# Attention summed by parts, and split projection weights kept in DRAM

## The chip, the core and the metric

The kernel runs on one core of a Trainium2 chip. The metric is the time of one execution in microseconds of the device (us), taken as the median of several runs. A core has a matrix engine (TensorE, PE in the profile; its weight loads are listed as PEld), a vector engine (VectorE, DVE), an activation engine (ScalarE, ACT), a general engine (GpSimd, POOL) and SyncE (SP), whose queue issues nearly all DMAs of this kernel. Work arrays lie in SBUF (128 partitions); matrix products land in PSUM.

## What is computed

One layer of a hybrid decoder block on 2048 tokens of width 1024, in float32. The normalised and modulated input `h` is projected by one matrix `w_in` of 4232 columns; the columns feed three mixers, whose gated outputs go through `w_out` and are added to the input.

```python
proj = h @ w_in                     # u, v, z of a gMLP; q, k, v, o, z, i, f of an mLSTM; q, k, v, z of attention
# stick-breaking attention, 6 heads of 64, by blocks of 128 queries:
z = einsum('bthd,bshd->bhts', qb, kb) * scale
log_not = where(strict, log_sigmoid(-z), 0.0)           # strict: s < t
suffix = cumsum(log_not, reverse=True) - log_not
a = where(strict, exp(log_sigmoid(z) + suffix), 0.0)
out = einsum('bhts,bshd->bthd', a, vb)
```

So the weight of key s is sigmoid(z_s) times the product of sigmoid(-z) over the later keys. With B_s, the product of sigmoid(-z) from s to the end, it is B_(s+1) - B_s.

## The kernel before, in words

The sequence is 16 tiles of 128 tokens, taken in three blocks of 5, 5 and 6 tiles (`BLOCKS`). For a block, the modulated input lies transposed in SBUF, split into a high and a low part (`hT`), and so do the projection's weights: every product with a projection is three matmuls, high by high, high by low and low by high.

**Weights.** `weights` yields the columns of one projection as 8 tiles of 128 rows (`wt`, tag `wr`, 11 buffers). `load_w` brings 256 rows into a staging tile (`st`, 2 buffers); ACT copies the high part, and DVE and POOL in turn subtract it to make the low part (L180, L181). A block calls it for 11 projections: three times q, k, v of a pair of heads (`c_proj`), and eight others. So every weight is loaded and split three times, once in a block: 33 calls, 264 tiles.

**Attention.** Heads are taken in pairs, p = 0, 1, 2. `c_proj` makes q, k and v of a pair, tile by tile; `c_evac` normalises q and k, turns them into `Qst` and `Kst` and puts v, high and low part, into `Vst`. It works in two pieces, the second one tile later. K and V of earlier blocks come from DRAM (`k_d`, `v_d`). `stick` then runs units (a query tile, a head, up to four key tiles, from the last keys to the first), 240 in all, in a pipeline of four steps: `front` makes the scores (PE), two sigmoids `bb` and `be` (ACT), masks the diagonal tile in both (POOL), runs the product from right to left over `bb` (a scan on DVE, 513 columns with a 1 at the end), and multiplies `be` by the shifted `bb`, in turn on DVE and POOL; `middle` transposes the result (PE) and splits it into `aT` (ACT high, DVE low); `back` multiplies with `Vst`; `fin` folds the parts and stores the tile (`yc`).

**Order.** While attention of a pair runs, the other projections of the block are woven between its steps (`interleave`, by estimated cost). The order on each engine comes from a scheduler that follows priorities: weights stand far ahead of the rest (`HIGH`), attention a little (`STK`). On the chip each engine and the SP queue then run their instructions in that fixed order. After the third block the output phase does the mLSTM's chunks and the output projection; nothing of the change is in it.

Of the kernel before, what the change touches and what calls it, by code (L numbers as in the profile page):

```python
# [17 lines left out]
P = 128  # L18
# [6 lines left out]
WMAX = 392  # L25
STK = -30
T5 = 6
OFF = dict(au=0, av=256, az=512, bq=768, bk=1152, bv=1536, bo=1920, bz=2304, bi=2688,
           cq=2696, ck=3080, cv=3464, cz=3848)
# [3 lines left out]
def hybrid_block_kernel(ctx: ExitStack, tc: tile.TileContext, x, c, norm_g, w_ada, b_ada, w_in,  # L33
# [8 lines left out]

# [1 line left out]
    qkT_d = dram.tile([768, SEQ], F32, name="qkT_d")  # L44
# [7 lines left out]
    k_d = [dram.tile([P, 2, SEQ], F32, name=f"k_d{p}") for p in range(3)]  # L52
    v_d = [dram.tile([P, NT, 2, P], F32, name=f"v_d{p}") for p in range(3)]

# [1 line left out]
    ident = const.tile([P, P], F32, name="ident")  # L56
# [35 lines left out]

# [1 line left out]
    rs = ExitStack()  # L94
# [50 lines left out]
    def mod_x(i, c0, c1, eng=None):  # L145
        """normalised and modulated, in place"""
        xc = x_cols(i, c0, c1)
        nc.vector.scalar_tensor_tensor(xc, xc, xtiles[i][1], hscale[:, c0:c1], ALU.mult, ALU.mult)
        (eng or nc.gpsimd).tensor_tensor(xc, xc, hshift[:, c0:c1], ALU.add)
# [10 lines left out]

    ntag = [0]

    def load_w(src, segs, kp):
# [8 lines left out]
    def weights(src, segs, kps=range(KT // 2), staged=None):  # L172
        """hi and lo parts of the given columns, one tile per 128 rows"""
        W = sum(w for _, w in segs)
        tiles = []
        for kp in kps:
            st = staged[kp] if staged else load_w(src, segs, kp)
            for a in range(2):
                wt = wr_p.tile([P, 2, WMAX], F32R, tag="wr", name=f"wr{ntag[0]}_{kp}_{a}")
                nc.scalar.copy(wt[:, 0, :W], st[:, a, :W])  # L180
                (nc.vector if a == 0 else nc.gpsimd).tensor_tensor(  # L181
                    wt[:, 1, :W], st[:, a, :W], wt[:, 0, :W].bitcast(F32), ALU.subtract)
                tiles.append(wt)
        ntag[0] += 1
        return tiles
# [4 lines left out]

# [1 line left out]
    ht_p = lw.enter_context(tc.tile_pool(name="ht", bufs=1))  # L192
# [4 lines left out]
    crow = tmp.tile([8, P], F32, tag="t512", bufs=T5, name="crow")  # L197
    brow = [stk.tile([P, 512], F32, tag="bb", bufs=4, name=f"brow{n}") for n in range(4)]
    for n in (2, 0, 3, 1):
        nc.gpsimd.memset(brow[n], 0.0)  # L200
    g_bc = [stk.tile([P, 512], F32, tag="be", bufs=3, name=f"g_bc{n}") for n in range(2)]

# [41 lines left out]

# [1 line left out]
    NB0 = BLOCKS[0]  # L246
# [22 lines left out]
    def hT_half(i, j, hh):  # L269
        """half of the rows of tile j of hT, hi and lo parts"""  # L270
        cols = slice(j * P, (j + 1) * P)
        ks = slice(hh * 4, hh * 4 + 4)
        pt = (pat.tile([P, 4, P], F32, tag="at", name=f"pt{i}_{hh}") if i < BLOCKS[0] else
              pproj.tile([P, 512], F32, tag="proj", name=f"pt{i}_{hh}").rearrange("p (k t) -> p k t", k=4))
        for k in range(4):
            kk = hh * 4 + k
            nc.tensor.transpose(pt[:, k, :], x_cols(i, kk * P, (kk + 1) * P), ident)
        nc.scalar.copy(hT[:, 0, ks, cols], pt)
        nc.vector.tensor_tensor(hT[:, 1, ks, cols], pt, hT[:, 0, ks, cols].bitcast(F32), ALU.subtract)  # L279

    def proj_tc(ps, wt, j, W, ks=range(KT)):
        """psum[t, cols] of t tile j of the block"""
        cols = slice(j * P, (j + 1) * P)
        for k in ks:
            nc.tensor.matmul(ps, lhsT=hT[:, 0, k, cols], rhs=wt[k][:, 0, :W], start=k == 0, stop=False)  # L285
            nc.tensor.matmul(ps, lhsT=hT[:, 0, k, cols], rhs=wt[k][:, 1, :W], start=False, stop=False)  # L286
            nc.tensor.matmul(ps, lhsT=hT[:, 1, k, cols], rhs=wt[k][:, 0, :W], start=False, stop=k == KT - 1)  # L287
            yield 3 * W / 2.4

# [1 line left out]
    def c_proj(b, t0, nb, p):  # L291
# [20 lines left out]
    def c_evac(b, t0, p, j, ps):  # L312
        i = t0 + j
        if p == 0:
# [7 lines left out]
        nc.gpsimd.tensor_tensor(rr, rr, neghalf[:, 0:4], ALU.pow)  # L322
        nc.scalar.copy(Vst[:, i, :, 0:64], ps[:, 256:384].rearrange("p (h d) -> p h d", h=2))
        nc.vector.tensor_tensor(Vst[:, i, :, 64:128], ps[:, 256:384].rearrange("p (h d) -> p h d", h=2),
                                Vst[:, i, :, 0:64].bitcast(F32), ALU.subtract)
        qk = tmp.tile([P, 4, 2, 64], F32, tag="t512", bufs=T5, name=f"qk{p}_{i}")
# [5 lines left out]
        for a in range(4):  # L332
# [7 lines left out]
        nc.vector.scalar_tensor_tensor(Qst[:, j, 1], pt[:, 0:2, :], gq, Qst[:, j, 0].bitcast(F32),  # L340
                                       ALU.mult, ALU.subtract)
        if b < len(BLOCKS) - 1:
            nc.sync.dma_start(k_d[p][:, :, i * P:(i + 1) * P], ks.bitcast(F32))
            nc.sync.dma_start(v_d[p][:, i], Vst[:, i].bitcast(F32))

    def stick(p, t0, nb):
# [11 lines left out]
        st = {}  # L358
        st_count = []

        def front(u):
# [6 lines left out]
            nc.tensor.matmul(z[:, :w], lhsT=Qst[:, j, 1, h, :], rhs=kk, start=False, stop=True)  # L368
            bb = stk.tile([P, 513], F32, tag="bb", bufs=4, name=f"bb{nm}")
            be = stk.tile([P, 512], F32, tag="be", bufs=3, name=f"be{nm}")  # L370
            nc.gpsimd.memset(bb[:, w:w + 1], 1.0)  # L371
            nc.scalar.activation(bb[:, :w], z[:, :w], AF.Sigmoid, scale=-1.0)  # L372
            nc.scalar.activation(be[:, :w], z[:, :w], AF.Sigmoid)  # L373
            if s1 == i + 1:
                nc.gpsimd.affine_select(out=bb[:, w - P:w], in_=bb[:, w - P:w], pattern=[[-1, P]],  # L375
                                        compare_op=ALU.is_gt, fill=1.0, base=0, channel_multiplier=1)
                nc.gpsimd.affine_select(out=be[:, w - P:w], in_=be[:, w - P:w], pattern=[[-1, P]],
                                        compare_op=ALU.is_gt, fill=0.0, base=0, channel_multiplier=1)
            rev = bb[:, 0:w + 1][:, ::-1]
            nc.vector.tensor_tensor_scan(rev, rev, rev, carry.get((i, h), 1.0), ALU.mult, ALU.bypass)  # L380
            carry[i, h] = bb[:, 0:1]
            eng = nc.gpsimd if len(st_count) % 2 else nc.vector
            st_count.append(0)
            eng.tensor_tensor(be[:, :w], be[:, :w], bb[:, 1:w + 1], ALU.mult)  # L384
            st[u] = [be, None]
            return 2 * w / 2.4

        def middle(u):
            i, j, h, s0, s1 = u
            nm = f"{p}_{i}_{h}_{s0}"  # L390
            be = st[u][0]
            nb_ = s1 - s0
            at = pat.tile([P, 4, P], F32, tag="at", name=f"at{nm}")
            for s in range(nb_):
                nc.tensor.transpose(at[:, s, :], be[:, s * P:(s + 1) * P], ident)  # L395
            aT = stk.tile([P, 4, 2, P], F32R, tag="aT", bufs=3, name=f"aT{nm}")
# [23 lines left out]
        def fin(u):  # L420
# [6 lines left out]
            yc = stk.tile([P, P], F32, tag="yc", bufs=1, name=f"yc{p}_{i}")  # L427
            nc.scalar.copy(yc, py[:, 0:P])
            nc.sync.dma_start(y_d[i * P:(i + 1) * P, 256 + p * P:256 + (p + 1) * P], yc)
# [10 lines left out]

# [1 line left out]
    def bqk_proj(t0, nb, half):  # L442
# [71 lines left out]

# [1 line left out]
    def a_proj(t0, nb, p):  # L516
# [37 lines left out]

# [1 line left out]
    def gating():  # L556
# [62 lines left out]

# [1 line left out]
    def bc4(ap, n):  # L621
# [31 lines left out]
    def first_chunk():  # L653
        """chunk 0 of the mLSTM ahead of the output phase: its gated output and the state after it"""
        big = [tmp.tile([P, D], F32, tag="xt", name=f"m0_{n}") for n in range(2)]
# [37 lines left out]

# [1 line left out]
    def gate_gemv():  # L695
# [137 lines left out]

# [1 line left out]
    rs.close()  # L835
# [46 lines left out]
    def mlstm(i):  # L882
        """numerator and denominator of chunk i, state after it"""
        qk2, vb = loaded[i][0:2]
# [31 lines left out]
    def mixed(i):  # L916
        """the gated outputs of the three mixers, [t, c]"""
        gt, y, xt = loaded[i][2:]
# [42 lines left out]
    def chunk_ahead(i):  # L961
        """chunk i from its scores to the turned outputs"""
        yield from mlstm(i)
        mixed(i)
        yield
        yield from turned(i)
# [66 lines left out]
```

## Time and profile before

| | |
|---|---|
| median of 3 runs | 1531.31 us (1530.76 to 1535.02) |
| span of the profiled execution, first to last instruction | 1527.0 us |
| instructions | 25375 |

The profiled execution's own time is known as its span; what lies around the span, the start and the end of the program, is taken as the difference to the median, 4.3 us. Stretches below are in us from the span's start. The first block runs to some 356 us (its last projection is mixed with the loading of the next block's x), the second to some 720, the third to 1262, and then the output phase. A share of busy time is an average; an engine's instruction can be busy and yet be held up by another's use of a resource.

### The profile page before, as it was taken

The page shows a single profiled execution, that of the slowest core. Times are in us where ns is not written, and L with a number is a line of the kernel's source. Part 1 is how long each engine was busy: PE and PEld are TensorE (multiplying, and loading weights), DVE is VectorE, ACT ScalarE, POOL GpSimd, SP SyncE. Part 2 cuts the span into 40 slices and gives each one's busy share as a digit, 9 for nine tenths or more (in the row PEclk, how much of TensorE's full clock was granted, in tenths as well). Part 3 has the DMA queues.
Part 4 walks back from the last instruction along what each step waited for, and adds up shares of the span by engine and source line. Part 5 has one row for each costly group of instructions (what it writes and reads, how often), then busy time and mean ns, then how long its engine had stood idle before and what let it go on. Part 6 is the DMA issues. An engine that isn't in the chain of part 4 may idle for free.

```text
span 1527.0 us, 25375 instructions
## 1 busy us (share of the span) xinstructions
PE 1413.2 (93%) x8468; PEld 1307.1 (86%) x8468; DVE 1123.3 (74%) x1866; ACT 749.6 (49%) x1832; POOL 757.2 (50%) x1228
## 2 busy tenths in 40 slices
PE   5899999889889999988898899999998978999998
PEld 3789999889878999977898699989898956888887
DVE  6787555775997677699699986879968797544444
ACT  2365444454655455557366755656545565211210
POOL 4364544664445544666344554645535246534442
PEclk8899999999999999999999999999999999999999
DMA  9433423334435422523322124112230154546551
GB/s 325 130 92 100 121 80 87 95 109 122 133 93 140 136 69 74 141 53 111 103 63 74 41 63 124 46 48 76 78 89 18 62 189 120 196 128 190 149 158 67
DMA packets 170595, 163.89 MB, mean 107 GB/s; under 512 B 23610, under 2 KB 146904, under 8 KB 170464
## 3 DMA queue, kind: packets, MB, share of 16 engines
q1 hardware_dynamic: 170240, 162.24, 36.1%
q8 instruction: 67, 1.10, 0.3%
q14 instruction: 64, 0.52, 0.1%
q0 software_dynamic: 224, 0.02, 0.0%
HBM read 124.58 MB, written 37.64 MB: 106 GB/s over the span
## 4 chain that ended last, share of the span: by engine, by line
PE 53%; DVE 25%; issue 7%; DMA 6%; POOL 5%; ACT 4%; SPq 0%; DVEq 0%; POOLq 0%; ACTq 0%
DVE bb L380 9%; PE po L946 4%; PE po L948 4%; PE po L947 4%; PE av L410 3%; PE pc L287 3%; DMA st<-in_w_in_dram 3%; PE pc L285 3%; PE pc L286 3%; PE at L395 3%; DVE acc L467 2%; DVE aT L398 2%; PE pg L286 2%; DVE be L384 2%; PE pg L285 2%
## 5 line engine op out<-in xcount | busy, mean ns | idle before, releaser
L380 DVE TENSOR_TENSOR_SCAN bb<-bb,bb 128x513 f32<-128x513 f32 x144 | 198.9, 1382 | 18.4 <-ACT bb L372 18.0
L384 POOL TENSOR_TENSOR be<-be,bb 128x512 f32<-128x512 f32 (+3 forms) x120 | 135.3, 1127 | 125.2 <-DVE bb L380 65.5
L181 POOL TENSOR_TENSOR wr<-st,wr 128x384 fp32r<-128x384 f32 (+1 forms) x132 | 158.4, 1204 | 61.8 <-ACT wr L180 60.0
L180 ACT CAST wr<-st 128x384 fp32r<-128x384 f32 (+1 forms) x264 | 127.3, 522 | 113.0 <-DMA st<-in_w_in_dram 103.2
L410 PE MATMUL av<-aT,Vst 128*128 128x256 f32 x816 | 148.1, 298 | 30.4 <-DVE aT L398 20.8
L410 PEld LDWEIGHTS av<-aT,Vst 128*128 128x128 f32 x816 | 120.6, 192 | 47.5 <-DVE aT L398 30.5
L398 DVE TENSOR_TENSOR aT<-at,aT 128x512 fp32r<-128x512 f32 (+3 forms) x240 | 142.0, 596 | 24.0 <-ACT aT L397 23.6
L372 ACT ACTIVATE bb<-z 128x512 f32<-128x512 f32 (+3 forms) x240 | 131.1, 547 | 53.4 <-PE z L368 47.4
L397 ACT CAST aT<-at 128x512 fp32r<-128x512 f32 (+3 forms) x240 | 126.8, 529 | 51.7 <-PE at L395 50.4
L395 PE MATMUL at<-ident,be 128*128 128x128 f32 x816 | 133.3, 278 | 16.6 <-DVE Qst L340 7.3
L285 PE MATMUL pc<-wr,hT 128*128 128x384 f32 (+1 forms) x384 | 136.0, 356 | 7.2 <-DVE hT L279 6.2
L287 PE MATMUL pc<-wr,hT 128*128 128x384 f32 (+1 forms) x384 | 136.8, 356 | 2.6 <-DVE hT L279 2.6
L181 DVE TENSOR_TENSOR wr<-st,wr 128x384 fp32r<-128x384 f32 (+1 forms) x132 | 103.9, 787 | 47.8 <-ACT wr L180 47.5
L286 PE MATMUL pc<-wr,hT 128*128 128x384 f32 (+1 forms) x384 | 134.7, 351 | 0.0
L373 ACT ACTIVATE be<-z 128x512 f32<-128x512 f32 (+3 forms) x240 | 132.6, 552 | 0.0
L395 PEld LDWEIGHTS at<-ident,be 128*128 128x128 f32 x816 | 98.4, 142 | 28.2 <-DVE aT L398 11.1
L380 DVE TENSOR_TENSOR_SCAN bb<-bb 128x129 f32<-128x129 f32 (+3 forms) x96 | 95.7, 997 | 17.4 <-POOL bb L375 14.5
L946 PE MATMUL po<-wo,yT 128*128 128x512 f32 x256 | 104.8, 409 | 0.3 <-ACT yT L935 0.3
L947 PE MATMUL po<-wo,yT 128*128 128x512 f32 x256 | 102.3, 399 | 0.7 <-POOL wo L853 0.7
L948 PE MATMUL po<-wo,yT 128*128 128x512 f32 x256 | 101.4, 399 | 0.0
L371 POOL MEMSET bb<- 128x1 f32 x240 | 23.4, 98 | 150.6 <-DVE bb L380 98.8
L367 PE MATMUL z<-Kst,Qst 128*128 128x512 f32 (+3 forms) x240 | 93.7, 392 | 3.8 <-ACT be L373 3.7
(272 smaller groups left out, 4098.7 us busy)
## 6 DMA issues: line engine op xcount, KB each, us to landing
st<-in_w_in_dram SPq DMA_DIRECT2D x180, 128.0 KB, 2.4
st<-in_w_in_dram SPq DMA_DIRECT2D x48, 384.0 KB, 3.3
st<-in_w_in_dram SPq DMA_DIRECT2D x48, 192.0 KB, 2.6
wad<-in_w_ada_dram SPq DMA_DIRECT2D x8, 1024.0 KB, 7.3
xo<-in_x_dram SPq DMA_DIRECT2D x16, 512.0 KB, 3.6
out_dram<-o SPq DMA_DIRECT2D x31, 256.0 KB, 2.8
xt<-in_x_dram SPq DMA_DIRECT2D x15, 512.0 KB, 4.4
qk<-qkT_d SPq DMA_DIRECT2D x15, 384.0 KB, 7.5
```

Source lines behind the costliest of these rows:

```text
L181: (nc.vector if a == 0 else nc.gpsimd).tensor_tensor(wt[:, 1, :W], st[:, a, :W], wt[:, 0, :W].bitcast(F32), ALU.subtract)
L285: nc.tensor.matmul(ps, lhsT=hT[:, 0, k, cols], rhs=wt[k][:, 0, :W], start=k == 0, stop=False)
L286: nc.tensor.matmul(ps, lhsT=hT[:, 0, k, cols], rhs=wt[k][:, 1, :W], start=False, stop=False)
L287: nc.tensor.matmul(ps, lhsT=hT[:, 1, k, cols], rhs=wt[k][:, 0, :W], start=False, stop=k == KT - 1)
L380: nc.vector.tensor_tensor_scan(rev, rev, rev, carry.get((i, h), 1.0), ALU.mult, ALU.bypass)
L384: eng.tensor_tensor(be[:, :w], be[:, :w], bb[:, 1:w + 1], ALU.mult)
L395: nc.tensor.transpose(at[:, s, :], be[:, s * P:(s + 1) * P], ident)
L398: nc.vector.tensor_tensor(aT[:, :nb_, 1, :], at[:, :nb_, :], aT[:, :nb_, 0, :].bitcast(F32), ALU.subtract)
L410: nc.tensor.matmul(flat(av), lhsT=Vst[:, s0 + s, h, :], rhs=flat(aT[:, s]), start=(s0 + s == i), stop=(s0 + s == 0))
L946: nc.tensor.matmul(po, lhsT=yT[:, 0, k, :], rhs=wo[k][:, 0, cs], start=k == 0, stop=False)
L947: nc.tensor.matmul(po, lhsT=yT[:, 0, k, :], rhs=wo[k][:, 1, cs], start=False, stop=False)
L948: nc.tensor.matmul(po, lhsT=yT[:, 1, k, :], rhs=wo[k][:, 0, cs], start=False, stop=k == KT - 1)
```

## The change

Attention: `be`, its mask and the product are left out. The weighted sum over s of (B_(s+1) - B_s) v_s is summed by parts: the output is v of the query's tile's last row plus the sum over s of B_s times (v_(s-1) - v_s). So `front` has one sigmoid and the scan, over 512 columns; `middle` transposes `bb` itself; `c_evac` puts the differences of neighbouring rows of v into `Vst`, for which a copy of v is moved by one partition with a DMA, and the first row comes from the last row of the tile before, through DRAM (`vl_d`); and `fin` adds the last row, spread over all partitions by a DMA (`vlast`).

Weights: the first block stores every split tile to DRAM; in the second and third block a tile is loaded from there, both parts at once, and staging and split are left out.

```diff
     def weights(src, segs, kps=range(KT // 2), staged=None):
         W = sum(w for _, w in segs)
         tiles = []
+        key = segs[0][0]
+        made = split.setdefault(key, {})
         for kp in kps:
+            if kp * 2 in made:
+                for k in (2 * kp, 2 * kp + 1):
+                    wt = wr_p.tile([P, 2, WMAX], F32R, tag="wr", name=f"wr{ntag[0]}_{k}")
+                    nc.sync.dma_start(wt[:, :, :W].bitcast(F32), made[k])
+                    tiles.append(wt)
+                continue
             st = staged[kp] if staged else load_w(src, segs, kp)
             for a in range(2):
                 wt = wr_p.tile([P, 2, WMAX], F32R, tag="wr", name=f"wr{ntag[0]}_{kp}_{a}")
...
+                made[2 * kp + a] = dram.tile([P, 2, W], F32, name=f"w_d{key}_{2 * kp + a}")
+                nc.sync.dma_start(made[2 * kp + a], wt[:, :, :W].bitcast(F32))
                 tiles.append(wt)
...
     def c_evac(b, t0, p, j, ps):
...
-        nc.scalar.copy(Vst[:, i, :, 0:64], ps[:, 256:384].rearrange("p (h d) -> p h d", h=2))
-        nc.vector.tensor_tensor(Vst[:, i, :, 64:128], ps[:, 256:384].rearrange("p (h d) -> p h d", h=2),
-                                Vst[:, i, :, 0:64].bitcast(F32), ALU.subtract)
+        vt = tmp.tile([P, P], F32, tag="vt", name=f"vt{p}_{i}")
+        nc.scalar.copy(vt, ps[:, 256:384])
+        nc.sync.dma_start(vl_d[p * NT + i:p * NT + i + 1, :], vt[P - 1:P, :])
+        dv = tmp.tile([P, P], F32, tag="dv", name=f"dv{p}_{i}")
+        nc.sync.dma_start(dv[1:P, :], vt[0:P - 1, :])
+        if i == 0:
+            nc.gpsimd.memset(dv[0:1, :], 0.0)
+        else:
+            nc.sync.dma_start(dv[0:1, :], vl_d[p * NT + i - 1:p * NT + i, :])
...
         yield
...
+        nc.gpsimd.tensor_tensor(dv, dv, vt, ALU.subtract)
+        dv2 = dv.rearrange("p (h d) -> p h d", h=2)
+        nc.scalar.copy(Vst[:, i, :, 0:64], dv2)
+        nc.gpsimd.tensor_tensor(Vst[:, i, :, 64:128], dv2, Vst[:, i, :, 0:64].bitcast(F32), ALU.subtract)
...
         def front(u):
...
-            bb = stk.tile([P, 513], F32, tag="bb", bufs=4, name=f"bb{nm}")
-            be = stk.tile([P, 512], F32, tag="be", bufs=3, name=f"be{nm}")
-            nc.gpsimd.memset(bb[:, w:w + 1], 1.0)
+            bb = stk.tile([P, 512], F32, tag="bb", bufs=BB, name=f"bb{nm}")
             nc.scalar.activation(bb[:, :w], z[:, :w], AF.Sigmoid, scale=-1.0)
-            nc.scalar.activation(be[:, :w], z[:, :w], AF.Sigmoid)
             if s1 == i + 1:
                 nc.gpsimd.affine_select(out=bb[:, w - P:w], in_=bb[:, w - P:w], pattern=[[-1, P]],
                                         compare_op=ALU.is_gt, fill=1.0, base=0, channel_multiplier=1)
-                nc.gpsimd.affine_select(out=be[:, w - P:w], in_=be[:, w - P:w], pattern=[[-1, P]],
-                                        compare_op=ALU.is_gt, fill=0.0, base=0, channel_multiplier=1)
-            rev = bb[:, 0:w + 1][:, ::-1]
+                if h == 0:
+                    vlast[i] = stk.tile([P, P], F32, tag="vlast", name=f"vlast{p}_{i}")
+                    nc.sync.dma_start(vlast[i], vl_d[p * NT + i:p * NT + i + 1, :].broadcast_to([P, P]))
+            rev = bb[:, 0:w][:, ::-1]
             nc.vector.tensor_tensor_scan(rev, rev, rev, carry.get((i, h), 1.0), ALU.mult, ALU.bypass)
             carry[i, h] = bb[:, 0:1]
-            eng = nc.gpsimd if len(st_count) % 2 else nc.vector
-            st_count.append(0)
-            eng.tensor_tensor(be[:, :w], be[:, :w], bb[:, 1:w + 1], ALU.mult)
-            st[u] = [be, None]
+            st[u] = [bb, None]
...
         def middle(u):
...
-                nc.tensor.transpose(at[:, s, :], be[:, s * P:(s + 1) * P], ident)
+                nc.tensor.transpose(at[:, s, :], bb[:, s * P:(s + 1) * P], ident)
...
         def fin(u):
...
-            nc.scalar.copy(yc, py[:, 0:P])
+            nc.vector.tensor_tensor(yc, py[:, 0:P], vlast.pop(i), ALU.add)
```

`BB` is 6; `vt` and `dv` have two buffers, `vlast` two. The start of the program uses `bb`'s buffers where it used `be`'s.

## Rows read from the trace of the kernel before

**Rows 1.** The page, busy time: us, share of the span, instructions.

```profile
PE 1413.2 (93%) x8468; PEld 1307.1 (86%) x8468; DVE 1123.3 (74%) x1866; ACT 749.6 (49%) x1832; POOL 757.2 (50%) x1228
```

**Rows 2.** Stretches: length, busy us (x) of PE, PEld, DVE, ACT, POOL; clock, DMA share, GB/s.

```profile
69.00:382.00 313.00, 298.01 (x1830) 289.56 (x1829) 209.03 (x400) 156.65 (x429) 165.98 (x287) 0.98 0.36 100
382.00:494.00 112.00, 99.56 (x632) 91.43 (x631) 101.79 (x160) 62.83 (x155) 58.50 (x102) 0.98 0.42 120
494.00:612.00 118.00, 118.00 (x736) 114.83 (x735) 85.47 (x144) 65.66 (x166) 56.89 (x103) 1.00 0.35 97
612.00:767.00 155.00, 138.66 (x838) 131.84 (x837) 121.81 (x202) 83.68 (x215) 88.21 (x139) 0.98 0.36 101
767.00:914.00 147.00, 134.31 (x811) 124.63 (x810) 134.89 (x207) 98.28 (x209) 69.56 (x125) 0.98 0.19 56
914.00:1086.00 172.00, 168.90 (x1076) 161.72 (x1075) 140.40 (x219) 105.48 (x249) 88.25 (x151) 1.00 0.24 68
1086.00:1216.00 130.00, 122.46 (x743) 116.32 (x742) 99.70 (x172) 70.19 (x178) 57.19 (x112) 0.97 0.22 61
1216.00:1262.00 46.00, 35.60 (x225) 28.47 (x224) 43.61 (x54) 31.69 (x68) 18.90 (x36) 0.96 0.53 189
1262.00:1527.00 265.00, 252.91 (x1428) 215.05 (x1428) 137.35 (x243) 54.18 (x127) 121.88 (x126) 0.98 0.48 145
```

**Rows 3.** What PE waits for from 316 to 1262 us: us in total, times, longest.

```profile
PE av L410 <- DVE aT L398: 20.0, 20, 2.6
...
PE pc L285 <- DVE hT L279: 6.2, 3, 4.8
...
PE pv L286 <- DVE wr L181: 2.6, 2, 2.4
```

**Rows 4.** The scan's line: durations in ns, min/median/max.

```profile
L380 DVE TENSOR_TENSOR_SCAN bb<-bb,bb x144: 1268/1278/3400, 114.7 to 1257.9; 128x513 f32<-128x513 f32 x144
```

**Rows 5.** Timeline from 716 us: start, duration, engine, line.

```profile
716.10 2.70 POOL L149 TENSOR_TENSOR xt<-xt,hshift 128x1024 f32<-128x1024 f32 x1
...
716.49 3.40 DVE L380 TENSOR_TENSOR_SCAN bb<-bb,bb 128x513 f32<-128x513 f32 x1
```

**Rows 6.** Groups of instructions: busy us, mean ns | idle before, releasers.

```profile
L373 ACT ACTIVATE be<-z 128x512 f32<-128x512 f32 (+3 forms) x240 | 132.6, 552 | 0.0
...
L416 DVE TENSOR_TENSOR avt<-av,avs 128x128 f32<-128x128 f32 x96 | 26.6, 277 | 25.3 <-ACT avs L414 25.1
...
L533 POOL TENSOR_TENSOR gu<-tb 128x128 f32<-128x128 f32 x32 | 19.8, 618 | 24.4 <-DVE tb L532 23.3 <-PE pa L287 0.8
...
L324 DVE TENSOR_TENSOR Vst<-pc,Vst 128x128 fp32r<-128x128 f32 x48 | 13.3, 281 | 2.1 <-ACT Vst L323 2.1
```

**Rows 7.** The product of be and bb alone: length, busy us (x) of DVE, POOL.

```profile
382.00:494.00 112.00, 6.69 (x12) 14.19 (x12) 0.98 0.42 120
767.00:914.00 147.00, 14.73 (x20) 24.43 (x19) 0.98 0.19 56
1216.00:1262.00 46.00, 6.87 (x9) 12.43 (x10) 0.96 0.53 189
```

**Rows 8.** The weights' low parts alone: the same columns.

```profile
382.00:494.00 112.00, 8.24 (x12) 16.77 (x12) 0.98 0.42 120
767.00:914.00 147.00, 10.73 (x12) 16.71 (x12) 0.98 0.19 56
```

**Rows 9.** The DMA view: queue's packets, MB, share; loads by size, us to landing.

```profile
q1 hardware_dynamic: 170240, 162.24, 36.1%
...
st<-in_w_in_dram SPq DMA_DIRECT2D x48, 384.0 KB, 3.3
st<-in_w_in_dram SPq DMA_DIRECT2D x48, 192.0 KB, 2.6
```

**Rows 10.** What the DMA queue on SP waits for: us, times, longest.

```profile
SPq L167 <- POOL wr L181: 171.4, 57, 32.4
```

**Rows 11.** One q-k-v projection of block 1: columns as in the stretches above.

```profile
494.00:519.00 25.00, 25.00 (x152) 24.46 (x151) 11.79 (x25) 9.71 (x27) 10.41 (x14) 1.00 0.50 150
```

More of the change, by code (lines that the diff above doesn't have):

```diff
@@ L27 @@
 T5 = 6
+BB = 6
 OFF = dict(au=0, av=256, az=512, bq=768, bk=1152, bv=1536, bo=1920, bz=2304, bi=2688,
@@ L53, in hybrid_block_kernel @@
     v_d = [dram.tile([P, NT, 2, P], F32, name=f"v_d{p}") for p in range(3)]
+    vl_d = dram.tile([3 * NT, P], F32, name="vl_d")
     ident = const.tile([P, P], F32, name="ident")
@@ L161, in hybrid_block_kernel @@
     ntag = [0]
+    split = {}
     def load_w(src, segs, kp):
@@ L197, in hybrid_block_kernel @@
     crow = tmp.tile([8, P], F32, tag="t512", bufs=T5, name="crow")
-    brow = [stk.tile([P, 512], F32, tag="bb", bufs=4, name=f"brow{n}") for n in range(4)]
+    brow = [stk.tile([P, 512], F32, tag="bb", bufs=BB, name=f"brow{n}") for n in range(4)]
     for n in (2, 0, 3, 1):
         nc.gpsimd.memset(brow[n], 0.0)
-    g_bc = [stk.tile([P, 512], F32, tag="be", bufs=3, name=f"g_bc{n}") for n in range(2)]
+    g_bc = [stk.tile([P, 512], F32, tag="bb", bufs=BB, name=f"g_bc{n}") for n in range(2)]
     def ada_load(half):
@@ L358, in stick @@
         st = {}
-        st_count = []
+        vlast = {}
         def front(u):
@@ L390, in middle @@
             nm = f"{p}_{i}_{h}_{s0}"
-            be = st[u][0]
+            bb = st[u][0]
             nb_ = s1 - s0
```

## The prediction

> **What bounds the kernel now.** I read the page's busy times first, then the busy times by stretch, then what TensorE waits for, then the timeline of one long wait. TensorE (PE) is busy for 93% of the span [rows 1], so its work, which the change leaves alone, sets a floor. The stretches say how far above it the kernel runs [rows 2]. In 494 to 612 us PE is busy all 118.0 us with 736 instructions: 0.160 us each, PE at its own pace. At that pace the other stretches would need, from their counts: 69 to 382, 293.4 of 313 us (19.6 over); 382 to 494, 101.3 of 112 (10.7); 612 to 767, 134.3 of 155 (20.7); 767 to 914, 130.0 of 147 (17.0); 914 to 1086, nothing over; 1086 to 1216, 119.1 of 130 (10.9); 1216 to 1262, 36.1 of 46 (9.9). Together 88 to 89 us that PE isn't at its pace. The output phase, 1262 to 1527, isn't touched.
>
> Three of these are VectorE's (DVE's): it is busy 101.8 of 112, 134.9 of 147 and 43.6 of 46 us, above PE's need in each. The waits agree: PE's largest is the `av` matmul for the low part `aT` that DVE makes, 20.0 us [rows 3]. In the other stretches over PE's pace DVE is at 0.67 to 0.79, and PE also waits for `hT` (6.2 us), which comes with a new block of x. Only few waits are for split weights (2.6 us in the largest row), so the splits harm PE through the engines that they occupy, not by being late.
>
> DVE is also longer at its work than the work takes. A scan of 513 columns has a median of 1278 ns and a maximum of 3400 [rows 4]. The timeline has that maximum: POOL's addition runs from 716.10 for 2.70 us, the scan starts at 716.49 and ends at 719.89, about 1.1 us after POOL [rows 5]. POOL work that reads SBUF can hold up a DVE instruction with two SBUF operands.
>
> **What the change removes.** (a) The second sigmoid, `be`: 240 ACT instructions, 132.6 us [rows 6]; ACT isn't the bound, so alone it is worth nothing, but the score buffer comes free one activation sooner. `bb` gets six buffers for its four and `be`'s three; it now lives until its transposes, one unit longer, which six cover. (b) The product of `be` and `bb`, every other one on DVE: 6.7, 14.7 and 6.9 us of DVE in the three DVE stretches, and 14.2, 24.4 and 12.4 us of POOL [rows 7]. (c) The second and third splits of the weights: in two of these stretches 8.2 and 10.7 us of DVE, 16.8 and 16.7 of POOL [rows 8]; the third has none.
>
> DVE's need falls to 101.8 - 6.7 - 8.2 = 86.9 us in the first and 134.9 - 14.7 - 10.7 = 109.5 in the second, both under PE's need (101.3 and 130.0), so their 10.7 and 17.0 us can come back whole; in the last, 43.6 - 6.9 = 36.7 us stays level with PE's 36.1, and I take 7 of 9.9. That is 35 us. The other stretches hold 51 us over PE's pace, in which DVE gets lighter but x's loads and the chain through `hT` stay, and block 0 keeps its splits. Bounds 0 and 51; no row parts them, so half, 26. Gain: 61 us.
>
> **What it adds.** (d) In the evacuation of q, k and v one DVE subtraction from PSUM (281 ns) goes, and the 48 additions of `vlast` come to DVE; the nearest, `avt`, takes 277 ns [rows 6]. Even. That addition can wait for its broadcast DMA, with the next scans queued behind it on DVE; four units lie between issue and use, so nothing. (e) POOL gets two subtractions of 128x128 per tile, 96 in all: at most the 618 ns of `gu` [rows 6], 59 us, less than (b) and (c) free. The first waits for the shifted copy; behind it on POOL stand the next tile's `rr` and the attention's selects.
>
> (f) **The weights in blocks 1 and 2** come as 176 tiles of 384 KB straight into `wr`, which has 11 buffers of which 8 are in use: three tiles ahead, where the staging held four more. One tile feeds three matmuls, 0.48 us. The fourth tile's buffer comes free 0.48 us into the last row tile of the projection before, and is wanted at 3.84 + 1.44 = 5.28 us. A 384 KB load lands 3.3 us after issue and one of 192 KB in 2.6 [rows 9], so a further tile costs about 2 x 0.7 = 1.4 us. The eighth lands at 0.48 + 3.3 + 4 x 1.4 = 9.4 us and is wanted at 7.2: 2.2 us late. Upper bound 22 x 2.2 = 48 us; lower 0, where attention's matmuls lie between a projection's, as in most stretches. I take eight, the six q-k-v projections and two more, 18 us, less 3 us of waits for splits that go [rows 3]: 15 us. Each load also waits in SP's queue behind whatever is there; SP stands up to 32.4 us at a weight load today, for a split [rows 10]. In block 0 the 88 stores (35 MB) follow the splits on the same queue; the queue moved 162.24 MB in 36.1% of the engines' time [rows 9], so they are 117 us of all 16 engines, and 69 to 382 us goes from a share of 0.36 to 0.73: still hidden, behind PE, and if that cover went a projection would start late as in the other blocks.
>
> (g) **The shift.** Per tile SP issues three more DMAs: the last row of v out, that row of the tile before in, and 127 rows of 512 B moved by one partition. No row has a DMA of 127 rows. By [rows 9], 0.361 x 16 x 1527.0 us over 170240 packets is 51.8 ns for a packet of 953 B, 18.4 B/ns for an engine. Spread over 16 engines the shift holds each 0.2 to 0.4 us; if one engine carries it, by bytes 3.5 us, by packets 6.6. A q-k-v projection of block 1 has five tiles in 25 us at a DMA share of 0.50 [rows 11]: that engine has 2.5 us of other work in a tile's 5.0. Lower bound of the cost 0; the upper is the second rival's. Its packets are the smallest kind, nearest to the lower end, where two buffers of `vt` and `dv` absorb most: I take 8 us.
>
> The Trainium skill (DMA: Bandwidth & Descriptors, "Why a DMA increments its semaphore by 16 and not by 1") says that a DMA uses the largest number of engines up to 16 that divides its slowest dimension, and names 127 partitions as using one. No row here shows it. By that rule the shift's row of the sum would lie between the 30 and 123 us of the second rival; by a spread over 16 it would be 0.
>
> **Sum.** -61 + 15 + 8 = -38 us on the profiled span of 1527.0: 1489, and with the 4.3 us by which the median of the runs (1531.31) stands above that span, **1493 us**.
>
> **Rivals.**
> 1. *All of the slack comes back and both DMA costs are hidden.* 35 + 51 = 86 us: 1445. For it: the stretch 494 to 612 shows that attention and projection can interleave at PE's pace with DVE at 0.72. Against: `hT` and x.
> 2. *The shift is the new bound, slower.* Place: the nine q-k-v projections. If one engine carries it, a tile needs 2.5 + 3.5 to 6.6 = 6.0 to 9.1 us of that engine in 5.0: 1.0 to 4.1 us over. POOL waits for `dv`, so `rr` of the next tiles, hence `qk` and the scores' operands, come late; the weights that follow on the same queue too. Two tiles in each of nine groups find free buffers; 30 are left: 30 to 123 us. It decides when it passes 61 - 15 = 46 us, 1.5 us a tile, a shift of 4.0 us. Middle: 76 - 46 = +30, 1561 us. Against: 512 B packets should be shorter than the mean one.
> 3. *The gain is eaten by the weights.* Every one of 22 projections 2.2 us late (48 us), and the 26 us do not come: -35 + 45 = +10, 1541 us. For it: three tiles of lead and SP's order. Against: attention's matmuls fill in.
> 4. *Costs and gain cancel:* 61 us against 30 for the shift (the lower end of rival 2) and 14 late projections, 31 us: 1531.
>
> **Chances.** What a measurement of this kernel can tell from no change is some 0.3%, 4.6 us. Forecast with its neighbourhood (1470 to 1520): 0.52. Rival 1: 0.15. Rival 4: 0.10, most of it within 0.3%. Rival 2: 0.15. Rival 3: 0.08. So faster 0.68, the same 0.08, slower 0.24. The range goes from rival 1 to a little past rival 3 and the lower part of rival 2: 1444 to 1550; for the forecast alone 1470 to 1520.
>
> **What would show it.** Right: in 382 to 494 and 767 to 914 PE reaches 0.160 us an instruction with DVE under 0.85; scans with few long ones; no wait of PE for `wr` above 2 us a projection; the shift landing in under 4 us. The sum is wrong if PE waits for `wr`<-DMA in sums of 30 us or more (rival 3), if POOL's idle time before the subtraction of `dv` adds up to tens of us and the q-k-v projections grow past 25 us (rival 2), or if DVE stays above 0.9 busy although lighter.

## The result, and the profile after

The changed kernel takes **1551.01 us** (median of four runs, 1548.09 to 1552.60) against 1533.16 for the kernel before on the same chip: a ratio of 1.0119, 95% interval [1.0098, 1.0140], slower by 1.2%. The forecast was 1493, with a range to 1550. The time lies 10 us from the middles of two rivals, 1541 of the third (the gain is eaten by the weights) and 1561 of the second (the shift is the new bound); the waits below tell them apart.

The page after has its busy times first (us, share of the span, instructions), then the main hardware queue's packets, MB and share of 16 engines, then the leading groups of the chain that ended last:

```profile
PE 1423.9 (92%) x8468; PEld 1318.7 (85%) x8468; DVE 942.6 (61%) x1658; ACT 577.4 (37%) x1416; POOL 490.2 (32%) x783
...
q1 hardware_dynamic: 199994, 237.90, 47.8%
...
PE av L429 4%; PE at L414 4%; PE po L965 3%; PE po L967 3%; PE po L966 3%; DMA dv<-vt 3%; DMA wr<-w_d 2%; DMA dv<-vl_d 2%; PE z L391 2%; PE z L392 2%; DVE bb L402 2%; PE pa L298 2%; PE pa L299 2%; PE pa L300 2%; PE pg L299 1%
```

Against [rows 1] the change did what it says: DVE lost 181 us of work, ACT 172, POOL 267; PE has the same 8468 instructions. The time still rose, and the chain names transfers of `dv`, a tile that the kernel before hasn't got. Two of the stretches of [rows 2] in which DVE stood above PE's need (same columns and the same times from the start of the span, so not quite the same work):

```profile
382.00:494.00 112.00, 104.60 (x665) 98.77 (x664) 82.69 (x149) 46.88 (x117) 26.33 (x56) 0.97 0.60 195
767.00:914.00 147.00, 136.54 (x819) 128.53 (x818) 105.98 (x185) 72.63 (x155) 29.80 (x62) 0.97 0.32 101
```

DVE is at 0.74 and 0.72 where it was at 0.91 and 0.92. What the engines wait for (us in total, times, longest) tells what took its place:

```profile
ACT Vst L364 <- POOL dv L362: 170.0, 44, 7.5
...
POOL dv L362 <- DMA dv<-vt: 93.5, 21, 8.6
...
POOL dv L362 <- DMA dv<-vl_d: 54.7, 17, 5.0
```

POOL stands 148 us, in 38 of 48 tiles, before the subtraction that needs the shifted copy; ACT stands 170 us behind POOL, 3.9 us a time. PE's largest wait is a new one, `PE pq L352 <- DVE qk L346: 14.0, 10, 3.9`: it waits to turn the scaled q and k (`qk`), which come late. For a stored weight it waits only 3.6 us at most at one place (`PE pb L472 <- DMA wr<-w_d`, 3.8 us in total), so it isn't the third rival.

**One place in detail**, the end of the second q-k-v projection of block 1. The timeline (start, duration, what; in brackets the idle time before and its releaser):

```profile
541.79 0.46 POOL L362 TENSOR_TENSOR dv<-dv,vt 128x128 f32<-128x128 f32 x1 [3.96 <-issue]
542.28 0.30 ACT L364 CAST Vst<-dv 128x128 fp32r<-128x128 f32 x1 [4.64 <-POOL dv L362]
542.48 0.38 ACT L331 ACTIVATE sq<-pc 128x256 f32<-128x256 f32 x1
542.65 0.47 POOL L365 TENSOR_TENSOR Vst<-dv,Vst 128x128 fp32r<-128x128 f32 x1 [0.41 <-ACT Vst L364]
...
543.15 0.34 SPq L368 DMA_DIRECT2D v_d<-Vst  x1
...
543.58 0.58 SPq L185 DMA_DIRECT2D wr<-w_d  x1
544.22 0.45 SPq L338 DMA_DIRECT2D vl_d<-vt  x1
544.72 0.69 DVE L346 TENSOR_TENSOR qk<-pc,rr 128x512 f32<-128x512 f32 x1 [1.41 <-POOL rr L335]
544.75 4.85 SPq L185 DMA_DIRECT2D wr<-w_d  x7
545.46 0.66 PE L352 MATMUL pq<-ident,qk 128*128 128x128 f32 x4 [1.59 <-DVE qk L346]
...
547.35 0.69 PE L298 MATMUL pg<-wr,hT 128*128 128x384 f32 x1 [0.88 <-DMA wr<-w_d]
...
549.56 0.69 PE L298 MATMUL pg<-wr,hT 128*128 128x384 f32 x1 [0.89 <-DMA wr<-w_d]
549.65 0.67 SPq L340 DMA_DIRECT2D dv<-vt  x1
...
558.87 0.46 POOL L362 TENSOR_TENSOR dv<-dv,vt 128x128 f32<-128x128 f32 x1 [6.11 <-DMA dv<-vt]
562.87 0.45 POOL L362 TENSOR_TENSOR dv<-dv,vt 128x128 f32<-128x128 f32 x1 [3.54 <-DMA dv<-vl_d]
...
563.35 0.30 ACT L364 CAST Vst<-dv 128x128 fp32r<-128x128 f32 x1 [2.57 <-POOL dv L362]
563.56 0.36 ACT L416 CAST aT<-at 128x256 fp32r<-128x256 f32 x1
...
563.96 0.42 DVE L417 TENSOR_TENSOR aT<-at,aT 128x256 fp32r<-128x256 f32 x1 [2.25 <-ACT aT L416]
...
564.43 0.79 PE L429 MATMUL av<-aT,Vst 128*128 128x256 f32 x2 [2.22 <-DVE aT L417]
```

The third tile's subtraction comes at 541.79, 5.3 us after its shift was issued (536.46). ACT's `Vst` cast has waited 4.64 us for it, and ACT is in order: the squares `sq` of the next tile stand behind the cast, then DVE's and POOL's `rr`, then `qk`, then PE at `pq`. SyncE's queue is in order too: it stands from 539.81 to 543.15 at the store `v_d<-Vst`, which needs POOL's last subtraction, and the weight loads of the next projection, `pg`, follow only then; PE waits for them 0.88 us at 547.35 and 0.89 at 549.56. In the whole run this store waits 23.0 us for POOL; by itself that can't be the loss, since a kernel below that loses nothing (128 unread rows) has 19.0 us of it.

The shift of the last tile but one goes out at 549.65, behind seven of these weight loads; POOL gets its `dv` 9.2 us later, and the last tile's 4 us after that. The cast `aT` of another unit stands behind the last `Vst` cast on ACT, DVE behind `aT`, and PE, at `av`, behind DVE. Now the same place in steps of 4 us (PE, PEld, DVE, ACT, POOL busy; granted clock, DMA share, GB/s):

```profile
544.00:548.00 4.00, 1.66 (x8) 1.34 (x9) 3.12 (x6) 1.79 (x6) 2.00 (x4) 0.92 0.77 223
548.00:552.00 4.00, 3.11 (x11) 2.44 (x10) 2.31 (x4) 0.00 (x0) 0.44 (x1) 0.50 0.92 302
552.00:556.00 4.00, 4.00 (x19) 3.77 (x19) 1.97 (x2) 0.98 (x2) 0.29 (x1) 0.73 0.84 309
556.00:560.00 4.00, 4.00 (x25) 3.88 (x24) 0.00 (x0) 0.64 (x3) 0.46 (x1) 1.00 0.15 42
560.00:564.00 4.00, 2.09 (x13) 1.56 (x11) 1.29 (x4) 1.43 (x6) 1.13 (x3) 1.00 0.15 42
564.00:568.00 4.00, 3.56 (x13) 3.57 (x14) 3.29 (x5) 2.52 (x6) 2.71 (x5) 0.57 0.39 123
```

Read PE's counts, not its busy time. PE idles 2.3 us of 544 to 548, at `pq` and `pg`, and the granted clock is 0.50 in the next step, the lower of its two levels (1.2 GHz): 11 instructions in 3.11 us of busy time where the step from 556, at full clock, has 25 in 4.00. It idles 1.9 us of 560 to 564, at that `av`, and the clock is 0.57 behind it. A wait is paid twice: as idle time, and as slower matmuls after it.

**The copy itself** shows in the DMA view where nothing else moves, 782 to 788 us in 40 slices of 0.15 us (busy share in tenths, then GB/s):

```profile
DMA  0000000000000000000000000000040000000000
GB/s 31 0 0 0 3 0 0 0 0 0 10 14 24 20 24 20 20 24 20 17 10 10 3 20 20 24 20 20 24 130 20 24 20 3 0 0 0 0 0 0
```

About 22 slices, 3.3 us, at 20 to 24 GB/s with a busy share that rounds to 0 of 16 engines: one engine's rate (the prediction's estimate from [rows 9] was 18.4 B/ns), while fifteen do nothing. The trace's packet records say the same: the 512 B packets take 27 ns each and nearly all start 22 to 42 ns apart, one after another.

### The profile page after: what moved, and what is told of

The parts are those of the page before. It is cut to its first block, busy times and chain, and to the rows that moved or that the text cites. A ratio compares the mean times of both kernels' runs of the same rounds, so it can differ in the third digit from the quotient of the medians.

```text
span 1548.7 us, 24164 instructions
## 1 busy us (share of the span) xinstructions
PE 1423.9 (92%) x8468; PEld 1318.7 (85%) x8468; DVE 942.6 (61%) x1658; ACT 577.4 (37%) x1416; POOL 490.2 (32%) x783
## 4 chain that ended last, share of the span: by engine, by line
PE 45%; DMA 9%; DVE 5%; issue 2%; ACT 2%; POOL 1%; SPq 1%; POOLq 0%; DVEq 0%; ACTq 0%
PE av L429 4%; PE at L414 4%; PE po L965 3%; PE po L967 3%; PE po L966 3%; DMA dv<-vt 3%; DMA wr<-w_d 2%; DMA dv<-vl_d 2%; PE z L391 2%; PE z L392 2%; DVE bb L402 2%; PE pa L298 2%; PE pa L299 2%; PE pa L300 2%; PE pg L299 1%
## 5 line engine op out<-in xcount | busy, mean ns | idle before, releaser
L402 DVE TENSOR_TENSOR_SCAN bb<-bb,bb 128x512 f32<-128x512 f32 x144 | 186.4, 1294 | 14.0 <-ACT bb L394 12.9
L429 PE MATMUL av<-aT,Vst 128*128 128x256 f32 x816 | 144.9, 292 | 14.4 <-DVE aT L417 8.9
L414 PE MATMUL at<-ident,bb 128*128 128x128 f32 x816 | 133.6, 277 | 9.5 <-DVE Qst L359 4.5
L298 PE MATMUL pc<-wr,hT 128*128 128x384 f32 (+1 forms) x384 | 135.6, 356 | 4.4 <-ACT hT L291 1.7
L300 PE MATMUL pc<-wr,hT 128*128 128x384 f32 (+1 forms) x384 | 133.1, 347 | 1.6 <-DVE hT L292 1.5
L299 PE MATMUL pc<-wr,hT 128*128 128x384 f32 (+1 forms) x384 | 132.9, 346 | 0.0
L414 PEld LDWEIGHTS at<-ident,bb 128*128 128x128 f32 x816 | 100.4, 143 | 18.4 <-DVE aT L417 6.5
L402 DVE TENSOR_TENSOR_SCAN bb<-bb 128x128 f32<-128x128 f32 (+3 forms) x96 | 88.9, 931 | 34.1 <-POOL bb L396 33.6
L472 PE MATMUL pb<-hT,wr 128*128 128x320 f32 (+1 forms) x288 | 95.8, 334 | 5.9 <-DMA wr<-w_d 3.8
L474 PE MATMUL pb<-hT,wr 128*128 128x320 f32 (+1 forms) x288 | 95.0, 332 | 2.8 <-POOL wr L192 2.7
L299 PE MATMUL pa<-wr,hT 128*128 128x384 f32 x256 | 90.6, 355 | 6.8 <-POOL wr L192 4.7
L473 PE MATMUL pb<-hT,wr 128*128 128x320 f32 (+1 forms) x288 | 95.3, 331 | 0.0
L298 PE MATMUL pa<-wr,hT 128*128 128x384 f32 x256 | 90.5, 355 | 4.3 <-DVE tb L551 3.0
L396 POOL TENSOR_SCALAR_AFFINE_SELECT bb<-bb 128x128 f32<-128x128 f32 x96 | 38.8, 408 | 174.7 <-ACT bb L394 156.1
```

Source lines behind the costliest of these rows:

```text
L414: nc.tensor.transpose(at[:, s, :], bb[:, s * P:(s + 1) * P], ident)
L429: nc.tensor.matmul(flat(av), lhsT=Vst[:, s0 + s, h, :], rhs=flat(aT[:, s]), start=(s0 + s == i), stop=(s0 + s == 0))
```

## The experiments

"Before" is the kernel before on the same chip: 1533.63 us in the first group, 1533.03, 1532.25, 1534.34 and 1532.47 in the later ones.

**Each half alone, and the shift in two pieces.** The first kernel has the attention alone, the second the weights alone; the third is the changed kernel, the fourth the attention alone, with this edit:

```diff
-        nc.sync.dma_start(dv[1:P, :], vt[0:P - 1, :])
+        nc.sync.dma_start(dv[1:113, :], vt[0:112, :])
+        nc.sync.dma_start(dv[113:P, :], vt[112:P - 1, :])
```

> Attention by parts alone; the weights are split in every block as before. Shift theory (the copy of 127 rows runs on one DMA engine, 3.3 us of it, and holds POOL and the start of each attention group): the loss is in this part, so some 1540 us, no better than before, with POOL's waits for dv again near 150 us. Weights theory (the stores in block 0 and the late loads afterwards cost it): this part alone shows its gain, 1490 to 1510 us.

> Weights kept in DRAM alone; attention as before. Shift theory: a gain from the splits that go, 1510 to 1525 us, and block 0 as long as before (316 us to its last projection). Weights theory: slower than before, 1545 to 1565 us, with block 0 longer by some 20 to 30 us.

> Both parts, the copy of 127 rows issued as two, 112 rows and 15 rows, one DMA more per tile and the same data. Shift theory: the copy lands about 3 us sooner, POOL's waits for dv fall from some 150 us to under 60, and the time to 1500 to 1520 us. Weights theory: nearly no change, 1540 to 1550 us.

> Attention by parts alone, with the copy as 112 and 15 rows. Shift theory: 20 to 40 us under the kernel with the copy of 127 rows, so 1500 to 1515 us. Weights theory: within 10 us of that kernel, both at 1490 to 1510 us.

Measured: attention alone 1570.28 us, ratio 1.0241 [1.0221, 1.0261]; weights alone 1481.64, 0.9661 [0.9635, 0.9688]; both with the shift in pieces **1470.23**, 0.9587 [0.9565, 0.9609]; attention alone with the shift in pieces 1492.20, 0.9731 [0.9716, 0.9746]. The same 127 rows as 112 and 15 are worth 81 us in the changed kernel and 78 in the attention alone. The shift theory has the sign right in all four and the size too small in all four. Page and waits of the kernel with both, shift in pieces:

```profile
PE 1394.2 (95%) x8468; PEld 1299.7 (88%) x8468; DVE 944.2 (64%) x1658; ACT 580.2 (40%) x1416; POOL 502.5 (34%) x783
...
POOL dv L363 <- DMA dv<-vt: 52.5, 25, 7.6
...
POOL dv L363 <- DMA dv<-vl_d: 5.7, 6, 2.3
```

POOL's waits for `dv` fall from 148 us to under 60. Of the 80.0 us between the two spans (1548.7 and 1468.7), 29.7 are PE busy time with the same instructions (1423.9 and 1394.2; mean granted clock 0.968 and 0.986, by which alone I estimate 26) and 50.3 are PE idle. PE's wait for `qk` falls from 14.0 to 4.3 us. At the place shown above (here 512 to 536 us) the weight loads run at full rate and PE doesn't stop:

```profile
512.00:516.00 4.00, 4.00 (x26) 3.92 (x25) 3.37 (x5) 1.84 (x6) 1.93 (x3) 1.00 1.04 347
516.00:520.00 4.00, 4.00 (x27) 3.84 (x26) 2.80 (x5) 1.82 (x4) 0.29 (x1) 1.00 1.05 365
520.00:524.00 4.00, 4.00 (x24) 3.92 (x23) 1.49 (x4) 2.17 (x7) 2.48 (x6) 1.00 0.34 94
```

**Is it the number of pieces or their sizes?** The cut moves to 113 and 14 rows, or to 126 and 1.

> Both parts, the copy as 113 and 14 rows. Theory of divisors (113 has no divisor up to 16 but 1, so one engine carries 113 rows, some 2.9 us of it): near the kernel with 127 rows, 1530 to 1550 us. Rival (two DMAs are faster than one because each is smaller): like 112 and 15 rows, 1465 to 1480 us.

> Both parts, the copy as 126 rows and 1 row. Theory of divisors (126 is 14 times 9): like 112 and 15, 1465 to 1480 us. If size alone counts, 126 rows are as slow as 127: 1530 to 1555 us.

Measured: 113 and 14 rows 1523.35 us, 0.9931 [0.9908, 0.9955]; 126 and 1 rows 1471.47, 0.9594 [0.9575, 0.9612]. Cutting isn't what helps. 112 and 126 have divisors between 2 and 16 (16 and 14), 113 and 127 are prime. The Trainium skill (DMA: Bandwidth & Descriptors, "Why a DMA increments its semaphore by 16 and not by 1") says that a transfer is spread over the largest number of engines, up to 16, that divides its slowest dimension; these four sizes agree with it. 113 rows cost 53 us where 127 cost 81, less than in proportion to the rows and under what was expected, though `dv` is as late: from `vt` to the subtraction 10.4 us on average with 113 rows, 10.1 with 127, 7.9 with 112 and 15. Why isn't settled.

**Late, or in the way?** Two kernels were to part the lateness of `dv` from the engine's occupation: 112 and 15 rows and one more 127-row copy of `vt` to DRAM that nobody reads; and no odd copy at all, `vt` going to DRAM whole and back one row earlier.

```diff
+        dx = dram.tile([P, P], F32, name=f"dx{p}_{i}")
+        nc.sync.dma_start(dx[1:P, :], vt[0:P - 1, :])
```

> Both parts with 112 and 15 rows, and beside them the copy of 127 rows once more, into a tile of DRAM that nothing reads. The engine is occupied as in the changed kernel, but dv isn't late. If occupation of the engine (the DMAs queued behind it) is what costs, 1530 to 1555 us; if the lateness of dv and POOL's wait for it is, 1470 to 1490 us.

> Both parts, v's tile stored to DRAM whole (128 rows) and read back one row earlier (128 rows): two transfers of 64 KB on 16 engines in a row, two DMAs a tile in place of three; the first tile of a pair alone is still copied as 112 and 15 rows. dv comes some 2 us later than with 112 and 15 rows, with no engine held. If lateness costs, 1510 to 1550 us; if occupation does, 1465 to 1485 us.

Measured: 1522.54 us, 0.9929 [0.9903, 0.9955], and 1473.54, 0.9611 [0.9586, 0.9635]. An unread copy costs 52 us; the time is in neither range. And it isn't a clean test: `dv`'s first row is issued behind it, and POOL waits 99.5 us for that row. Nor was the way over DRAM very late: the least time from `vt` to the subtraction was 3.4 us against 3.1 with pieces and 5.5 in the changed kernel (from the trace's `vt` copies and subtractions).

**Another queue, no shift, the stores alone.**

```diff
-        nc.sync.dma_start(dv[1:P, :], vt[0:P - 1, :])
+        nc.scalar.dma_start(dv[1:P, :], vt[0:P - 1, :])
```

> The changed kernel, its 127-row copy on one DMA engine issued from ScalarE's queue instead of SyncE's; the other transfers stay where they are. Theory 1 (what costs is that SyncE's queue goes on in order behind the copy): only those who need dv wait, 1470 to 1500 us. Theory 2 (the one engine itself is what is full, whichever queue fills it): within 15 us of the changed kernel, 1535 to 1560 us. Between the two: each has a share.

> The same with the copy as 112 and 15 rows on ScalarE's queue: what the move to that queue costs by itself. Both theories: within 8 us of the 112 and 15 rows on SyncE's queue, 1465 to 1478 us; if issuing from ScalarE is dear (48 tiles, 2 DMAs each, ScalarE 577 us busy), up to 1490.

> The changed kernel without the shift: dv is made on GpSimd as vt minus vt, so no DMA brings neighbouring rows and the differences are left out; all else, the last rows to DRAM too, stays. If copies on several engines cost nothing: 1463 to 1473 us, as with 112 and 15 rows. If they still cost as priced before the change (8 us): about 1462. If they hide a larger wait: 1440 to 1455.

> The kernel before with the split weights also stored to DRAM in the first block, and nothing read back: every block splits again. If the stores stand in the way of the first block's loads (as the rival of the eaten gain has it): 1540 to 1560 us. If they are hidden: 1530 to 1537 us.

Measured: 127 rows on ScalarE's queue **1569.26** us, 1.0245 [1.0226, 1.0263]; 112 and 15 there 1472.26, 0.9606 [0.9588, 0.9623]; no shift 1468.47, 0.9579 [0.9551, 0.9606]; stores alone 1533.06, 1.0005 [0.9989, 1.0020]. With 127 rows the time is above both ranges: moving the copy to another queue makes it 18 us worse, so what costs isn't the copy's own place in SyncE's queue. PE's wait for `qk` grows to 20.6 us. The run gives the price of a copy, since nothing else is on that queue (packets, MB, share of 16 engines), here with the waits:

```profile
q10 hardware_dynamic: 6144, 3.12, 0.7%
...
POOL dv L362 <- DMA dv<-vt: 99.7, 28, 8.3
```

0.007 x 16 x 1566.8 us over 48 copies is 3.7 us of one engine. The queue of the kernel with 112 and 15 rows shows 0.8%, no less engine time, but spread. Without any shift, and with the differences left out, the kernel is within 2 us of the one with pieces: spread, the shift is free within the noise. So are the stores of 35 MB in block 0.

**Occupied by something unrelated.** 127 or 128 rows of the constant `ident` to DRAM per tile, unread, on either queue; and, for lateness alone, one more hop on the way over DRAM.

```diff
+        dx0 = dram.tile([P, P], F32, name=f"dx0_{p}_{i}")
+        nc.scalar.dma_start(dx0[1:P, :], ident[0:P - 1, :])
```

> The fixed kernel (copy as 112 and 15 rows, 1470 us) with one more copy for each of the 48 tiles: 127 rows of a constant, the identity, to DRAM, which nobody reads, no buffer is held by, and no transfer of dv stands behind in its own tile. If occupation of one engine is what costs: 1500 to 1530 us. If only the lateness of dv costs: 1468 to 1480 us.

> The same unread 127 rows, issued on ScalarE's queue, so that nothing stands behind them in SyncE's queue. If the engine is shared between the queues and its time is what is short: as on SyncE's queue, 1500 to 1530 us. If what costs is the order within one queue: 1468 to 1480 us.

> Control: the same unread copy with 128 rows on SyncE's queue, the same bytes and issue, on 16 engines. Both theories: 1467 to 1476 us.

> No copy of 127 rows at all, but dv later: the v tile goes to DRAM, from there one row shifted to another place in DRAM, and from there to dv, each with 128 rows on 16 engines; the least time from vt to the subtraction should rise from 3.1 us to about 5.5 us, that of the changed kernel. If lateness of dv is what costs: 1500 to 1550 us. If occupation of one engine is: 1470 to 1485 us.

Measured: 127 rows 1600.75 us on SyncE's queue and 1604.97 on ScalarE's, 1.0443 [1.0418, 1.0468] and 1.0468 [1.0443, 1.0492]; 128 rows 1481.00, 0.9656 [0.9629, 0.9683]; three hops 1490.31, 0.9718 [0.9679, 0.9756]. The first two, above both ranges, don't answer the question: having nothing to wait for, the 48 copies all ran in the first 190 us and held up the start of the kernel, while the later stages took as long as with pieces. What they show is the rate at which such copies follow each other, by the issues' durations (ns, min/median/max), first 127 rows on ScalarE's queue, then 128 rows on SyncE's:

```profile
L347 ACTq DMA_DIRECT2D dx<-ident x48: 202/2954/10974, 1.9 to 179.6; - x48
```

```profile
L347 SPq DMA_DIRECT2D dx<-ident x48: 320/430/507, 27.8 to 67.9; - x48
```

2.95 us each against 0.43, and the issuing queue itself is held for that time. With three hops, between the two ranges, the least time to the subtraction is 6.1 us, the mean 11.1 (changed kernel 5.5 and 10.1), and it costs 20 us over the pieces. It isn't quite clean, since SyncE's queue stands 78.6 us for the hops (48.7 in the kernel over DRAM, which costs 3). So lateness as great as the changed kernel's is worth about 20 of the 81, if that wait is nearly free.

**Occupied, tile by tile.** The unread copy is taken from the tile's finished differences, so that it starts only after its own `dv` has been used; beside it a control with 128 rows.

```diff
+        dx = dram.tile([P, P], F32, name=f"dx{p}_{i}")
+        nc.sync.dma_start(dx[0:127, :], Vst[0:127, i, 0, :].bitcast(F32))
```

> The fixed kernel (112 and 15 rows, 1470 us) with one more copy per tile that nobody reads: 127 rows of the tile's finished differences to DRAM, which can start only once the tile's dv has arrived and been used, so the tile's own dv can't stand behind it, and the copies are spread over the tiles. If one engine taken for 3 us per tile costs by itself: 1495 to 1530 us. If what costs is a late dv: 1468 to 1482 us.

> Control: the same unread copy with 128 rows, on 16 engines. Both theories: 1470 to 1480 us.

Measured: 127 rows 1508.53 us, 0.9849 [0.9822, 0.9876]; 128 rows 1472.30, 0.9609 [0.9592, 0.9627]. One row less makes a copy that nobody needs cost 36 us. Its waits, then the control's:

```profile
ACT Vst L365 <- POOL dv L363: 72.6, 33, 7.3
...
POOL dv L363 <- DMA dv<-vl_d: 43.8, 17, 11.4
```

```profile
ACT Vst L365 <- POOL dv L363: 45.4, 30, 5.5
...
POOL dv L363 <- DMA dv<-vl_d: 17.2, 11, 3.0
```

POOL now waits up to 11.4 us for the first row of `dv`, a transfer of 512 B. On average `dv` is little later than in the control (9.2 against 8.3 us from `vt` to the subtraction), far less late than with three hops, and it costs more.

## Why the prediction was wrong

**The step that failed is (g), the shift: "I take 8 us".** The runs put 81 us in its place, by the same copy in 112 and 15 rows. The choice between the ends was made by the packets' size and by two buffers of `vt` and `dv`. But a packet's size doesn't tell how many engines carry the 127 rows, which is what had to be decided first (nor is 512 B the smallest kind: the page before has 23610 packets below it). The rule of the Trainium skill, written beside the sum, pointed to the second rival, yet that rival got a chance of 0.15. No row of before could test the rule; the four sizes now do.

**Rival 2 had the mechanism, but not all of its ways.** One engine, POOL's wait for `dv`, `rr` and `qk` late behind it: all in the rows above. But it was priced by that engine's throughput: by its reckoning a copy of 3.3 to 3.7 us costs 24 to 36 us and decides only from 4.0 us on. It cost 81 (and its landing in under 4 us was to show the forecast right). That 81 lies near the rival's middle of 76 is luck. Missing was ACT, which waits in order at its cast and brings the next tile's `qk` and other units' `aT` late; missing too was the clock that falls behind PE's pauses: 29.7 of the 80.0 us are the same matmuls run slower. An engine occupied without need costs 36 us (127 against 128 unread rows), a late `dv` about 20; the two overlap, since the unread rows also make `dv` a little late, and how the 81 us divide stays open.

**Its place was wrong.** The q-k-v projections were to grow past 25 us. The one of [rows 11] takes 24.1 us (518.4 to 542.5) where it took 24.5. Summed from PE's records, from the first matmul of each projection to the first of the next, the q-k-v projections take 290.8 us after and 290.3 before; the kernel with pieces, 276.7, is 14 us below both. The projections behind them (`pb`, `pg`, `pa`) take 20, 26 and 21 us more than with pieces: the late `dv` of the last tiles, and what stands behind it on ACT and in SyncE's queue, land there, as at the place above.

**The gain was sized about right.** With the shift free the kernel gains 63.4 us (1533.63 to 1470.23). The forecast without (g) was 61 - 15 = 46. The two stretches from which 10.7 and 17.0 us were to come back, taken with pieces from the first matmul of `pb` to that of the next q-k-v projection:

```profile
385.70:488.70 103.00, 97.63 (x643) 91.39 (x641) 75.50 (x133) 45.26 (x107) 23.16 (x49) 1.00 0.51 163
744.40:877.50 133.10, 131.48 (x835) 125.84 (x834) 109.82 (x184) 74.61 (x153) 25.54 (x53) 1.00 0.33 106
```

Before they last 112.4 us (382.3 to 494.7) and 147.6 (767.0 to 914.6), so 9.4 and 14.5 come back, PE is at 0.160 and 0.159 us an instruction and DVE at 0.73 and 0.83: the prediction's signs of being right. With the shift whole it is 105.6 and 142.2 us. Of the 17 us between 46 and 63, (f) can hold most, though no run parts it: the stores are hidden, as argued (+0.8 us, nothing by its interval), and PE's waits for stored weights sum to under 10 us, with the shift whole or in pieces, where 15 net were taken. The weights alone give -52.0 us, the attention alone with pieces -41.4, together 63, not 93. The likely reason is the first step of the prediction, PE's own work as the floor (95% busy), but no run tests it; nor is it parted which of the lightened engines, DVE, ACT or POOL, pays.

**Smaller points.** Of the 144 long scans 7 took over 2 us before, 1 after and 2 with pieces (maxima 3400, 2843 and 3098 ns): few, as forecast, but not none. The `vlast` addition and the longer life of `bb` show no wait among the largest; (e)'s subtractions take 0.46 us each, under the 0.618 taken.

The kernel with both parts and the shift as 112 and 15 rows, 1470.23 us, beats both kernels; 126 and 1 rows, 1471.47, is its equal.

## What to carry to other kernels

Before a DMA is priced, find how many engines can carry it: 127 rows of 512 B took one engine for over 3 us and 113 rows were dear too, 112, 126 or 128 weren't, and cutting the 127 into 112 and 15 made the change 5% faster. Such a transfer is paid by others: 127 rows that nobody reads cost 36 us more than 128. So its price is read from the waits of the others, and moving it to another queue made it dearer here (1569 against 1551 us). On an engine or a queue that works in order, a late transfer holds up all that stands behind its wait, and PE's pause is paid again in its clock (0.50 behind the pause at 544).

## What the runs showed of the hardware

A one-engine copy held the queue that issued it: back to back, 2.95 us an issue against 0.43 with 128 rows, and 48 of them at the start cost 120 us more than 48 of 128 rows (1600.75 against 1481.00 on SyncE's queue). A copy nobody reads cost 36 us for being one row short of 128. And the same 8468 PE instructions were busy 1394.2 us or 1423.9, at a mean granted clock of 0.986 or 0.968, with no change in PE's work.
